# Query projection and expert stage of a PEER feed-forward: five top-16 searches at another place, and pair sums searched among 112 candidates instead of 256

## The chip, the cores and the metric

One core of one Trainium2 chip. The metric is the time of one execution on the device in microseconds (us), taken as the median of several runs. The engines are TensorE (PE, with its weight loads as PEld), VectorE (DVE), ScalarE (ACT), GpSimd (POOL) and SyncE (SP, which issues transfers). Each works through its own instructions in the order in which the program emitted them.

## The reference, cut to what matters

A small network on 512 tokens of width 1024: a Mamba-2 layer, then a sliding-window attention layer, each followed by a PEER feed-forward and a gated embedding. The change is inside the PEER feed-forward, which runs twice:

```python
q = (h @ q_w).reshape(T, 8, 2, 128)                    # 8 heads, two halves
s = einsum('thcd,ckd->thck', q, sub_keys)              # 128 scores for each half
s1, i1 = top_k(s[:, :, 0], 16); s2, i2 = top_k(s[:, :, 1], 16)
cand_s = (s1[..., :, None] + s2[..., None, :])         # 16 x 16 pair sums
best_s, best_pos = top_k(cand_s.reshape(..., 256), 16)
idx = i1[best_pos // 16] * 128 + i2[best_pos % 16]     # 16 experts of 16384, for each head
gate = softmax(best_s)
a = einsum('nd,nhkd->nhk', h, u[idx]); w = gate * gelu(a)
out = einsum('nhk,nhkd->nd', w, v[idx])
```

Both lists s1 and s2 come out sorted, largest first.

## The kernel before, in words

Tokens are in four tiles of 128 (tile 0 to 3). For tile 0 the experts' rows are fetched one by one ("gather"): 128 rows of u and 128 rows of v for each token. For tiles 1 to 3 the whole table of 16384 experts is gone through in 128 **steps** (loop at the end of `peer`): step j streams 128 experts' weights, multiplies them with the 384 tokens (24 matmuls of 128x384, each product in three passes over high and low parts), applies gelu and writes the result GA. A later loop of 128 steps does the same with v.

A streamed weight block comes by SP's transfer (`ahead`, L150), ACT writes its high part `whi` (L169) and POOL its low part `wlo` in four pieces of 256 columns (L172); this is done two blocks ahead.

**Query projection.** 16 columns c of 128 outputs, two for each head. In the round of column c the program emits `lin`, a normalization step `napply` for rounds 3 to 11 (DVE `nf` L760, ACT `hhi` L764; eight of them on DVE, the last in round 10), the score matmuls of the column before (L971) with ACT's copies into `early` (tiles 0 and 3) and `late` (tiles 1 and 2), one call of `step()`, and ACT's copy of the column (`ga`, L966). `step()` takes the next item of the background generator, `bg_topk`: as soon as both halves of head h are there, in round 2h+2, the searches of tiles 0 and 3 for that head. In the odd rounds it has nothing to do.

**A search** (`topk`, `top16`) on DVE: for both halves MAX8, FIND_INDEX8, MATCH_REPLACE8, MAX8, FIND_INDEX8 over 128 columns, then one add that forms the 256 pair sums `cand` (L805), then the same five over them.

**Background of the expert steps** (`bg`). A list of items in a fixed order: T is a search (price 6.0), D a decode of one tile's positions into expert numbers (0.3, 5.0, 5.0 and 0.8), G one onehot (1.5): for four tokens two 128x1024 products on DVE, `early` (L884) and `og` (L886), and one item later 8 small matmuls and a copy (`gmm`, L898, L899). Each of the 128 steps adds 2.65 to a credit, and items are emitted while it is positive. Before, the walk through the list emits the last onehot in step 106.

**Gather.** The decode of tile 0 gives the row numbers `eg`; when two more items have been emitted (`late` is 2), `gi` is set to 0, and from the next step on each step makes 1.17 gather steps: DVE multiplies a fetched row with the activations (L678) and POOL issues the fetch of the row four ahead (L695), on the same queue as the `wlo` pieces. Five row buffers are in turn use. Before, the first gather step is in step 7.

PE waits for DVE in two ways: directly, where `gmm` needs a onehot, and through POOL, where a row's fetch waits until DVE has used the buffer and `wlo` pieces stand behind it.

Of the kernel before, what the change touches and what calls it, by code (L numbers as in the profile page):

```python
# [11 lines left out]
F32 = _mybir.dt.float32  # L12
# [3 lines left out]
U32 = _mybir.dt.uint32  # L16
AF = _mybir.ActivationFunctionType
OP = _mybir.AluOpType
AX = _mybir.AxisListType

P = 128
NT = 512
D = 1024
# [7 lines left out]
NJ = HEADS * TOPK  # L31
LAG = 4
LOP = 4
PAIR = (5, 6)
QT = 4
GSCALE = 32768.0
# [26 lines left out]
class Net:  # L63
# [576 lines left out]
    def peer(self, L):  # L640
# [106 lines left out]
        with ExitStack() as ctx:  # L747
# [46 lines left out]
            def topk(jobs):  # L794
                v = {}
                one, two = [], []
                for n, (tt, hd) in enumerate(jobs):
                    v[n] = mp.tile([P, 2, TOPK], F32, name=f"tv{n}")
                    for c in range(2):
                        src = early[hd][:, first.index(tt), c] if tt in first else late[:, later.index(tt), hd, c]  # L800
                        one.append((src, v[n][:, c, :], idx[:, c, tt, hd, :]))
                top16(one)
                for n, (tt, hd) in enumerate(jobs):
                    cand = mp.tile([P, TOPK, TOPK], F32, name=f"cand{n}", bufs=1)
                    vt.tensor_tensor(cand, v[n][:, 0, :, None].to_broadcast([P, TOPK, TOPK]),  # L805
                                     v[n][:, 1, None, :].to_broadcast([P, TOPK, TOPK]), op=OP.add)
                    two.append((cand.rearrange("p a b -> p (a b)"), best[:, tt, hd, :], pos[:, tt, hd, :]))
                top16(two)

            HK = HEADS * TOPK  # L810
# [5 lines left out]
            def decode_g(tt):  # L816
                gt = mp.tile([P, HEADS, TOPK], F32, name="gt", bufs=1)
                vt.tensor_tensor(gt, best[:, tt], best[:, tt, :, 0:1].to_broadcast([P, HEADS, TOPK]), op=OP.subtract)
                dec[tt] = gt, []
                return lambda: nc.scalar.activation(gt, gt, AF.Exp, scale=self.rv[:, tt:tt + 1])  # L820

            def decode_i(tt, c):
                pi = mp.tile([P, HEADS, TOPK], U32, name="pi", bufs=1)
                if c == 0:
                    vt.tensor_single_scalar(pi, pos[:, tt], 4, op=OP.logical_shift_right)
                else:
                    vt.tensor_single_scalar(pi, pos[:, tt], 15, op=OP.bitwise_and)
                pb = mp.tile([P, TOPK, HEADS], F16, name="pb", bufs=1)
                vt.tensor_copy(pb, pi.rearrange("p h k -> p k h"))
                ib = mp.tile([P, TOPK, HEADS], F16, name="ib")  # L830
                vt.tensor_copy(ib, idx[:, c, tt].rearrange("p h a -> p a h"))
                eq = mp.tile([P, TOPK, HK], F16, name="eq", bufs=1)
                vt.tensor_tensor(eq.rearrange("p a (n q) -> p a n q", q=QT),  # L833
                                 fl(pb).rearrange("p (n q) -> p n q", q=QT)[:, None].to_broadcast([P, TOPK, HK // QT, QT]),
                                 i16[:, :, None, :].to_broadcast([P, TOPK, HK // QT, QT]), op=OP.is_equal)
                e4 = eq.rearrange("p a (k h) -> p a k h", h=HEADS)
                vt.tensor_tensor(e4, e4, ib[:, :, None, :].to_broadcast([P, TOPK, TOPK, HEADS]), op=OP.mult)  # L837
                n = TOPK // 2
                while n > 1:
                    vt.tensor_tensor(eq[:, :n], eq[:, :n], eq[:, n:2 * n], op=OP.add)  # L840
                    n //= 2
                f = mp.tile([P, HK], F32, name=f"fi{c}", bufs=1)
                vt.tensor_tensor(f, eq[:, 0], eq[:, 1], op=OP.add)
                dec[tt][1].append(f)

            def decode_e(tt):
                gt, fi = dec.pop(tt)
                sm = mp.tile([P, 2, HEADS], F32, name="sm")
                vt.tensor_reduce(sm[:, 0], gt, axis=AX.X, op=OP.add)
                vt.reciprocal(sm[:, 1], sm[:, 0])  # L850
                gk = mp.tile([P, TOPK, HEADS], F32, name="gk", bufs=1)
                vt.tensor_tensor(gk, gt.rearrange("p h k -> p k h"), sm[:, 1, None, :].to_broadcast([P, TOPK, HEADS]),
                                 op=OP.mult)
                if tt == 0:
                    ef = wg[:, 0]
                    vt.tensor_scalar(ef, fi[0], float(P), float(L * NBLK * P), op0=OP.mult, op1=OP.add)
                    vt.tensor_tensor(ef, ef, fi[1], op=OP.add)
                    vt.tensor_copy(eg, ef)
                    vt.tensor_copy(gate, fl(gk))

                def turn():
                    if tt == 0:
                        self.gi = 0
                        return
                    pt = self.bank(7)
                    for j, src in enumerate(fi + [fl(gk)]):
                        nc.tensor.transpose(pt[:, j * P:(j + 1) * P], src, self.ident)
                    ts = slice(tt * P - NG, (tt + 1) * P - NG)
                    two = lambda j: pt[:, j * P:(j + 1) * P, None].to_broadcast([P, P, 2])
                    for j in range(2):  # L870
                        nc.scalar.activation(iT[:, ts, j], two(j), AF.Copy)
                    nc.scalar.activation(gT[:, ts, 0], two(2), AF.Copy, scale=GSCALE)
                    vt.scalar_tensor_tensor(gT[:, ts, 1], two(2), GSCALE, gT[:, ts, 0], op0=OP.mult, op1=OP.subtract)
                return turn
# [29 lines left out]
            def bg_topk():  # L904
                done = 0
                for hd in range(HEADS):
                    while self.hready <= hd:
                        yield
                    topk([(tt, hd) for tt in first])
                    yield  # L910

            def bg():
                items = []

                def T(tt, *hds):
                    for hd in hds:
                        items.append((6.0, lambda hd=hd: topk([(tt, hd)])))

                def D(tt):
                    items.append((0.3, lambda: decode_g(tt), 2))  # L920
                    items.append((5.0, lambda: decode_i(tt, 0)))
                    items.append((5.0, lambda: decode_i(tt, 1)))
                    items.append((0.8, lambda: decode_e(tt), 2))

                def G_(tt, lo, hi):
# [2 lines left out]
                        return lambda: gmm(b, o)  # L928
                    for b in range(32 * tt + lo, 32 * tt + hi):
                        items.append((1.5, lambda b=b: one(b)))  # L930
                D(0), T(1, 0, 1), D(3), T(1, 2, 3, 4), G_(3, 0, 12), T(1, 5, 6), G_(3, 12, 20), T(1, 7), D(1)
                G_(3, 20, 28), T(2, 0), G_(3, 28, 32), T(2, 1), G_(1, 0, 4), T(2, 2), G_(1, 4, 8), T(2, 3)
                G_(1, 8, 12), T(2, 4), G_(1, 12, 16), T(2, 5), G_(1, 16, 20), T(2, 6), G_(1, 20, 22), T(2, 7), D(2)
                G_(1, 22, 32), G_(2, 0, 32)
# [622 lines left out]
```

## Time and profile before

| what | us |
|---|---|
| median of 3 runs | 3457.02 (3456.63 to 3461.01) |
| the profiled execution, its own time | 3453.39 |
| its span, first to last instruction | 3451.6 |
| busy in the span: PE, DVE, POOL, ACT | 3291.1, 2672.6, 1953.3, 1455.2 |
| mean granted TensorE clock | 0.983 of full speed |
| first layer: query projection | 540 to 645 |
| first layer: expert steps (u) | 645 to 1283 |
| first layer: second expert loop (v) | 1285 to 1840 |
| second layer: projection, expert steps | 2100 to 2205, 2205 to 2845 |

The profiled execution is 3.6 us under the median. Line numbers (L805) are those of the kernel before. "Busy" of PE counts overlapping matmuls, so its share is no measure of its peak. Times in rows count from the start of the span.

### The profile page before, as it was taken

What the parts mean: (1) busy time and instruction counts of PE and PEld (TensorE: products, weight loads), DVE (VectorE), ACT (ScalarE), POOL (GpSimd) and SP (SyncE); (2) the same over time, 40 slices, a digit from 0 to 9 for tenths busy, and PEclk for the clock granted to TensorE, in tenths of its full rate; (3) what the DMA queues carried; (4) which work ended last, traced back from release to release, by engine and by line L of the source; (5) the groups of instructions that cost most, each with busy time, mean ns of one, the idle gap of its engine ahead of it and who ended that gap; (6) DMA issues with size and microseconds to landing.
All of it is one profiled execution on the core that took longest, in us unless ns stands there. A gap on an engine that the chain in (4) does not pass through costs nothing.

```text
span 3451.6 us, 52253 instructions
## 1 busy us (share of the span) xinstructions
PE 3291.1 (95%) x18814; PEld 3022.6 (88%) x18814; DVE 2672.6 (77%) x4880; ACT 1455.2 (42%) x2198; POOL 1953.3 (57%) x2168
## 2 busy tenths in 40 slices
PE   8999999989999999999998999999999999999997
PEld 5777777989998989999996668989998989999996
DVE  7667667899998737878777865899988737877775
ACT  4433434444445533333334553444445533333334
POOL 5444545789888884322217226688888884322214
PEclk9999999999999999999999999999999999999998
DMA  3222212488888999999983112488888989999982
GB/s 119 85 77 70 74 62 75 151 280 309 309 312 303 330 310 358 358 336 346 337 286 107 45 59 89 138 278 308 316 309 297 334 304 356 353 346 339 339 304 85
DMA packets 357300, 827.50 MB, mean 240 GB/s; under 512 B 30000, under 2 KB 196528, under 8 KB 350896
## 3 DMA queue, kind: packets, MB, share of 16 engines
q1 hardware_dynamic: 235136, 448.59, 40.3%
q0 software_dynamic: 73728, 268.47, 21.1%
q10 hardware_dynamic: 48176, 107.10, 8.2%
q8 instruction: 147, 2.41, 0.3%
q14 instruction: 113, 0.93, 0.1%
HBM read 717.09 MB, written 106.95 MB: 239 GB/s over the span
## 4 chain that ended last, share of the span: by engine, by line
PE 58%; DVE 25%; POOL 7%; issue 5%; DMA 4%; ACT 1%; SPq 0%; POOLq 0%; DVEq 0%; ACTq 0%
PE bank L202 17%; PE bank L203 17%; PE bank L204 17%; POOL wlo L172 6%; DVE row L678 4%; DVE early L884 3%; DVE og L886 2%; DMA row<-u,eg 2%; POOL row L695 2%; DVE eq L840 1%; PE bank L898 1%; DMA wraw<-ut 1%; PE bank L971 1%; DVE eq L833 1%; DVE eq L837 1%
## 5 line engine op out<-in xcount | busy, mean ns | idle before, releaser
L172 POOL TENSOR_TENSOR wlo<-wraw,whi 128x256 fp32r<-128x256 f32 x1564 | 1256.1, 835 | 564.4 <-ACT whi L169 513.1
L169 ACT ACTIVATE whi<-wraw 128x1024 fp32r<-128x1024 f32 x647 | 685.5, 1061 | 740.5 <-issue 316.3
L695 POOL DMA_INDIRECT row<-v,eg x256 | 310.0, 1211 | 716.8 <-DVE yg L687 700.2
L204 PE MATMUL bank<-hhi,wlo 128*128 128x384 f32 x2048 | 699.8, 342 | 13.3 <-POOL wlo L172 13.2
L202 PE MATMUL bank<-hhi,whi 128*128 128x384 f32 x2048 | 708.6, 346 | 0.7 <-ACT whi L169 0.7
L203 PE MATMUL bank<-hlo,whi 128*128 128x384 f32 x2048 | 697.3, 340 | 0.0
L203 PE MATMUL bank<-vlo,whi 128*128 128x384 f32 x2032 | 684.1, 337 | 6.1 <-DVE vlo L744 6.0
L202 PE MATMUL bank<-vhi,whi 128*128 128x384 f32 x2032 | 684.8, 337 | 0.8 <-ACT vhi L742 0.8
L204 PE MATMUL bank<-vhi,wlo 128*128 128x384 f32 x2032 | 683.6, 336 | 0.0
L172 DVE TENSOR_TENSOR wlo<-wraw,whi 128x1024 fp32r<-128x1024 f32 x256 | 313.3, 1224 | 148.6 <-ACT whi L169 147.5
L204 PEld LDWEIGHTS bank<-hhi,wlo 128*128 128x128 f32 x2048 | 392.0, 191 | 20.0 <-POOL wlo L172 19.8
L202 PEld LDWEIGHTS bank<-hhi,whi 128*128 128x128 f32 x2048 | 393.3, 192 | 1.0 <-ACT whi L169 1.0
L203 PEld LDWEIGHTS bank<-hlo,whi 128*128 128x128 f32 x2048 | 392.8, 192 | 0.0
L203 PEld LDWEIGHTS bank<-vlo,whi 128*128 128x128 f32 x2032 | 382.6, 188 | 8.2 <-DVE vlo L744 8.2
L202 PEld LDWEIGHTS bank<-vhi,whi 128*128 128x128 f32 x2032 | 382.6, 188 | 2.0 <-ACT vhi L742 1.5
L204 PEld LDWEIGHTS bank<-vhi,wlo 128*128 128x128 f32 x2032 | 382.4, 188 | 0.3 <-POOL wlo L172 0.3
L678 DVE SCALAR_TENSOR_TENSOR row<-row,pair 128x1024 f32<-128x1024 f32 x256 | 305.6, 1212 | 88.1 <-DMA row<-u,eg 87.6
L687 DVE SCALAR_TENSOR_TENSOR yg<-row,wg,yg 128x1024 f32<-128x1024 f32 x254 | 328.0, 1291 | 35.9 <-DMA row<-v,eg 35.8
L202 PE MATMUL bank<-z,whi 128*128 128x512 f32 x728 | 322.0, 442 | 3.4 <-DVE sg L1137 3.4
L695 POOL DMA_INDIRECT row<-u,eg x256 | 278.5, 1088 | 50.4 <-issue 29.1
L993 ACT ACTIVATE ga<-bank 128x384 f32<-128x384 f32 x256 | 125.3, 490 | 418.0 <-PE bank L204 409.0
L203 PE MATMUL bank<-z,whi 128*128 128x512 f32 x728 | 291.1, 400 | 4.7 <-DVE z L262 4.7
(322 smaller groups left out, 4863.6 us busy)
## 6 DMA issues: line engine op xcount, KB each, us to landing
wraw<-ut SPq DMA_DIRECT2D x256, 512.0 KB
wraw<-v SPq DMA_DIRECT2D x256, 512.0 KB
wraw<-wlin SPq DMA_DIRECT2D x135, 512.0 KB
GA<-ga ACTq DMA_DIRECT2D x256, 192.0 KB
G<-gsz ACTq DMA_DIRECT2D x48, 1024.0 KB
gv<-G SPq DMA_DIRECT2D x96, 512.0 KB
gsz<-GA SPq DMA_DIRECT2D x256, 192.0 KB
PJ<-nf ACTq DMA_DIRECT2D x16, 256.0 KB
```

The source lines that it names most:

```text
L169: nc.scalar.activation(hi, r, AF.Copy)
L172: self.lo_eng.tensor_tensor(lo[:, q:q + n], r[:, q:q + n], hi.bitcast(F32)[:, q:q + n], op=OP.subtract)
L202: mm(out, whi, xhi, start=start, stop=False)
L203: mm(out, whi, xlo, start=False, stop=False)
L204: mm(out, wlo, xhi, start=False, stop=stop)
L678: vt.scalar_tensor_tensor(r, r, 1.0, self.pair, op0=OP.mult, op1=OP.mult, accum_out=wg[:, 0, j:j + 1])
L687: vt.scalar_tensor_tensor(yg, r, wg[:, 0, j:j + 1], yg, op0=OP.mult, op1=OP.add)
L695: nc.gpsimd.indirect_dma_start(out=got[i], out_offset=None, in_=t["u"] if i < NJ else t["v"].rearrange("a p d -> (a p) d"), in_offset=bass ...
L833: vt.tensor_tensor(eq.rearrange("p a (n q) -> p a n q", q=QT), fl(pb).rearrange("p (n q) -> p n q", q=QT)[:, None].to_broadcast([P, TOPK, ...
L884: vt.tensor_tensor(pairs(o), iota.rearrange("p (a d) -> p a d", d=2)[:, None, None].to_broadcast([P, QT, 2, P // 2, 2]), alike(iT), op=OP. ...
L886: vt.tensor_tensor(pairs(og), pairs(o)[:, :, 0:1].to_broadcast([P, QT, 2, P // 2, 2]), alike(gT), op=OP.mult)
L993: nc.scalar.activation(ga[:, NG:], ps[:, NG:], AF.Gelu)
```

## The change

The pair sums are formed for the first four entries of the first list with all 16 of the second (64), and for the other twelve with the first four of the second (48): 112 columns from two adds instead of 256 from one. A position is then decoded differently, with one more DVE instruction in either half of a decode. In the query projection, the rounds after the searches of heads 2 to 6 search one head (0 to 4) of tile 1. The background list of the expert steps loses these five searches and begins with the decodes of tiles 0 and 3. Prices and credit stay.

```diff
+QEARLY = 5
...
-                    cand = mp.tile([P, TOPK, TOPK], F32, name=f"cand{n}", bufs=1)
-                    vt.tensor_tensor(cand, v[n][:, 0, :, None].to_broadcast([P, TOPK, TOPK]),
-                                     v[n][:, 1, None, :].to_broadcast([P, TOPK, TOPK]), op=OP.add)
-                    two.append((cand.rearrange("p a b -> p (a b)"), best[:, tt, hd, :], pos[:, tt, hd, :]))
+                    cand = mp.tile([P, 4 * TOPK + 4 * (TOPK - 4)], F32, name=f"cand{n}", bufs=1)
+                    for a, m, w in ((0, 4, TOPK), (4, TOPK - 4, 4)):
+                        o = cand[:, TOPK * a:TOPK * a + m * w].rearrange("p (a b) -> p a b", b=w)
+                        vt.tensor_tensor(o, v[n][:, 0, a:a + m, None].to_broadcast([P, m, w]),
+                                         v[n][:, 1, None, :w].to_broadcast([P, m, w]), op=OP.add)
+                    two.append((cand, best[:, tt, hd, :], pos[:, tt, hd, :]))
...
+                pb = mp.tile([P, TOPK, HEADS], F16, name=f"pb{c}", bufs=1)
+                turned = lambda x: x.rearrange("p h k -> p k h")
                 if c == 0:
+                    pk = mp.tile([P, HEADS, TOPK], U32, name="pk", bufs=1)
                     vt.tensor_single_scalar(pi, pos[:, tt], 4, op=OP.logical_shift_right)
+                    vt.tensor_single_scalar(pk, pos[:, tt], 2, op=OP.logical_shift_right)
+                    vt.scalar_tensor_tensor(pb, turned(pk), -12.0, turned(pi), op0=OP.add, op1=OP.max)
+                    dec[tt][2].append(pb)
                 else:
-                    vt.tensor_single_scalar(pi, pos[:, tt], 15, op=OP.bitwise_and)
-                pb = mp.tile([P, TOPK, HEADS], F16, name="pb", bufs=1)
-                vt.tensor_copy(pb, pi.rearrange("p h k -> p k h"))
+                    pa, pm = dec[tt][2][0], pi.bitcast(F32).rearrange("p h k -> p (h k)").rearrange(
+                        "p (k h) -> p k h", h=HEADS)
+                    vt.tensor_scalar(pm, pa, 4.0, 48.0, op0=OP.mult, op1=OP.add)
+                    vt.scalar_tensor_tensor(pm, pa, 16.0, pm, op0=OP.mult, op1=OP.min)
+                    vt.tensor_tensor(pb, turned(pos[:, tt]), pm, op=OP.subtract)
...
                     topk([(tt, hd) for tt in first])
                     yield
+                    if 2 <= hd < 2 + QEARLY:
+                        topk([(1, hd - 2)])
+                        yield
...
-                D(0), T(1, 0, 1), D(3), T(1, 2, 3, 4), G_(3, 0, 12), T(1, 5, 6), G_(3, 12, 20), T(1, 7), D(1)
+                D(0), D(3), T(1, 5, 6), G_(3, 0, 12), T(1, 7), G_(3, 12, 20), D(1)
                 G_(3, 20, 28), T(2, 0), G_(3, 28, 32), T(2, 1), G_(1, 0, 4), T(2, 2), G_(1, 4, 8), T(2, 3)
                 G_(1, 8, 12), T(2, 4), G_(1, 12, 16), T(2, 5), G_(1, 16, 20), T(2, 6), G_(1, 20, 22), T(2, 7), D(2)
                 G_(1, 22, 32), G_(2, 0, 32)
```

## Rows read from the trace of the kernel before

**Rows 1.** Busy us of each engine in three stretches of the expert steps; clock, DMA last.

```profile
645.00:1190.00 545.00, 507.65 (x3330) 494.73 (x3329) 508.61 (x964) 271.45 (x338) 476.26 (x544) 0.97 0.86 297
1190.00:1285.00 95.00, 90.91 (x512) 86.75 (x511) 32.30 (x44) 33.85 (x45) 84.12 (x103) 1.00 0.91 315
...
2205.00:2756.00 551.00, 515.40 (x3381) 502.75 (x3380) 497.50 (x971) 275.64 (x343) 483.58 (x552) 0.97 0.85 299
```

**Rows 2.** The chain that ended last, by line, from 645 to 868 us.

```profile
by line: DVE row L678 17.5%; DVE early L884 13.6%; DVE eq L840 7.1%; DVE og L886 6.9%; DVE eq L837 3.9%; DVE eq L833 3.6%; PE bank L202 3.0%; PE bank L204 2.8%; PE bank L203 2.8%; DVE idx L790 2.4%; PE bank L898 2.4%; DVE pos L787 2.2%; DVE
```

**Rows 3.** DVE in order of time, first layer (start us, us, engine line op).

```profile
651.76 0.63 DVE L818 TENSOR_TENSOR gt<-best 128x128 f32<-128x128 f32 x1
...
672.48 0.47 DVE L786 MAX8 tv<-gv 128x8 f32<-128x128 f32 x2
...
683.56 0.27 DVE L818 TENSOR_TENSOR gt<-best 128x128 f32<-128x128 f32 x1
...
699.10 1.22 DVE L678 SCALAR_TENSOR_TENSOR row<-row,pair 128x1024 f32<-128x1024 f32 x1
...
703.69 0.47 DVE L786 MAX8 tv<-gv 128x8 f32<-128x128 f32 x2
...
708.86 1.20 DVE L678 SCALAR_TENSOR_TENSOR row<-row,pair 128x1024 f32<-128x1024 f32 x1
...
1185.62 1.04 DVE L886 TENSOR_TENSOR og<-early,gT 128x1024 f16<-128x1024 f16 x1
```

**Rows 4.** ACT's gelu at the end of steps 14, 15, 20, 22, 107, 108, 127.

```profile
700.86 0.49 ACT L993 ACTIVATE ga<-bank 128x384 f32<-128x384 f32 x1 [2.15 <-PE bank L204]
709.29 0.49 ACT L993 ACTIVATE ga<-bank 128x384 f32<-128x384 f32 x1 [6.39 <-PE bank L204]
...
730.42 0.49 ACT L993 ACTIVATE ga<-bank 128x384 f32<-128x384 f32 x1 [2.15 <-PE bank L204]
...
748.41 0.49 ACT L993 ACTIVATE ga<-bank 128x384 f32<-128x384 f32 x1 [3.11 <-PE bank L204]
...
1189.31 0.49 ACT L993 ACTIVATE ga<-bank 128x384 f32<-128x384 f32 x1 [2.28 <-PE bank L204]
...
1193.47 0.49 ACT L993 ACTIVATE ga<-bank 128x384 f32<-128x384 f32 x1 [2.15 <-PE bank L204]
...
1279.54 0.49 ACT L993 ACTIVATE ga<-bank 128x384 f32<-128x384 f32 x1 [0.81 <-PE bank L204]
```

**Rows 5.** DVE groups by form, 645 to 1190 us; L301 is of the whole span.

```profile
L786 DVE MAX8 tv<-gv 128x8 f32<-128x128 f32 x32 | 7.7, 280 | 0.0
L786 DVE MAX8 best<-cand 128x8 f32<-128x256 f32 x18 | 7.6, 427 | 0.5
L805 DVE TENSOR_TENSOR cand<-tv 128x256 f32<-128x256 f32 x18 | 10.0, 560 | 0.0
L825 DVE TENSOR_SCALAR pi<-pos 128x128 uint32<-128x128 uint32 x4 | 2.0, 488 | 0.0
L678 DVE SCALAR_TENSOR_TENSOR row<-row,pair 128x1024 f32<-128x1024 f32 x115 | 136.8, 1211 | 3.4 <-DMA row<-u,eg 3.4
...
L301 DVE TENSOR_TENSOR rst<-rst 128x4 f32<-128x4 f32 x30 | 4.9, 163 | 1.0
```

**Rows 6.** The shortest kind of that add, in DVE's order of time, and POOL's pieces of `wlo`.

```profile
706.03 0.40 DVE L805 TENSOR_TENSOR cand<-tv 128x256 f32<-128x256 f32 x1
...
L172 POOL TENSOR_TENSOR wlo<-wraw,whi 128x256 fp32r<-128x256 f32 x1564 | 1256.1, 835 | 564.4 <-ACT whi L169 513.1
```

**Rows 7.** DVE in the query projection: two heads' first search instructions, and the normalization between.

```profile
592.21 0.68 DVE L786 MAX8 tv<-early 128x8 f32<-128x128 f32 x3 [2.16 <-ACT early L976]
...
601.63 1.12 DVE L760 SCALAR_TENSOR_TENSOR nf<-x,cols,rs 128x384 f32<-128x384 f32 x2
...
605.44 0.68 DVE L786 MAX8 tv<-early 128x8 f32<-128x128 f32 x3 [2.16 <-ACT early L976]
```

**Rows 8.** POOL's first row fetch, first layer.

```profile
673.34 1.11 POOL L695 DMA_INDIRECT row<-u,eg  x1 [0.16 <-DVE idx L787]
```

More of the change, by code (lines that the diff above doesn't have):

```diff
@@ L818, in decode_g @@
                 vt.tensor_tensor(gt, best[:, tt], best[:, tt, :, 0:1].to_broadcast([P, HEADS, TOPK]), op=OP.subtract)
-                dec[tt] = gt, []
+                dec[tt] = gt, [], []
                 return lambda: nc.scalar.activation(gt, gt, AF.Exp, scale=self.rv[:, tt:tt + 1])
@@ L846, in decode_e @@
             def decode_e(tt):
-                gt, fi = dec.pop(tt)
+                gt, fi, _ = dec.pop(tt)
                 sm = mp.tile([P, 2, HEADS], F32, name="sm")
```

## The prediction

> **What bounds the kernel now.** I read the stage table first, then the chain, then DVE's and ACT's order of time. PE looks full everywhere, but the table [rows 1] shows where it waits for something else: from 645 to 1190 us DVE is busy 508.6 of 545 us and PE's clock is below full (0.97, the mark of short stops), while from 1190 to 1285 DVE needs 32 of 95. In the second layer it is the same, a little less tight (497.5 of 551). The chain of the first 220 us runs through DVE's lines in turn, PE's have a tenth [rows 2]. In DVE's order of time nothing separates its instructions: from the first decode at 651.76 to the last onehot at 1186.6 [rows 3] it always has something waiting. So up to the last onehot DVE sets the end. After it, the steps run without background.
>
> PE's own pace is read from the gelu at the end of each step [rows 4]: a step without onehots takes 4.16 us (1189.31 to 1193.47); step 15 took 8.43, steps 21 and 22 together 18.0. PE does not wait for searches or decodes as such, it pays for DVE's arrears when it meets a late onehot or a late weight block. The last 20 steps take 90.2 us, 4.51 each (1189.31 to 1279.54).
>
> **The change part by part**, for one layer; both layers run the same code.
>
> *Five searches leave the expert steps.* Those of heads 0 and 1 took 672.48 to 683.56, 11.1 us; the next took 703.69 to 708.86, 5.17, and two more the same: 26.6 us off DVE [rows 3].
>
> *Eleven searches stay and get shorter.* MAX8 takes 280 ns over 128 columns and 427 over 256 [rows 5], 1.15 ns a column, so 144 columns fewer save 0.165 us; I take the other four of the five for alike: 0.83. The add becomes two. Its shortest row is 0.40 us [rows 6], an add of 4 columns takes 0.163 [rows 5], so one of 64 has 0.22 and one of 48 0.20 if nothing is in the way. In this stretch the add has a mean of 0.56, 0.16 over its shortest; giving each new one that wait, the two cost 0.74, 0.18 more. Saved: 0.65 a search, 7.2 in all. Without any wait it would be 0.80 and 8.8.
>
> *Four decodes have two instructions more each*, of 128 columns. The nearest row is a decode's shift, 0.488 [rows 5]: 1.0 a decode, 3.9 in all. The bounds are nothing, if the replaced conversions waited more, and twice that.
>
> *The five searches on DVE in the projection.* Two searches, two normalization steps and the wait for the next scores make a cycle of 13.23 us (592.21 to 605.44), of which 2.2 to 2.4 is waiting [rows 7]: PE's two columns set it. Now 1.3 goes (two searches), 4.7 comes (a search of 5.3 less 0.65): 16.6, less what closes of the wait, so 14.2 to 16.6, and I take 15. A normalization step stands behind the added search only for heads 2 and 3, because the eighth and last is in round 10. ACT's `hhi` waits for it, and behind `hhi` on ACT stand the copies to `early`, `ga` and `whi`, for which the score matmuls and POOL wait. Weights are two blocks ahead, 13 us, which hides 3.6 us (two cycles of 1.8 too much); if that cover were gone, PE would lose those 3.6. For heads 4 to 6 the cycle is about even. The last pair of searches saves 1.3, so DVE comes to the first decode 2.3 later. Bounds: 1.3 earlier, 4.5 later.
>
> *Rows.* The gather now begins in step 5, not 7. On POOL the first fetch [rows 8] moves ahead of two blocks' `wlo` pieces and waits there for the row numbers, which DVE has at the end of the first decode (672.48, now 675.8). POOL would come to it about 8.3 us earlier, so two blocks are held up for some 10 us, two steps of which are in reserve: PE stops for 2 to 4 us near step 8. I count nothing, because DVE has the longer queue at the first onehot; without that cover it costs these 4. On SP only the first loads of G start earlier, with the end of the background, beside steps that have DMA at 0.91 already [rows 1].
>
> *The order.* The list loses 30 of its credit, and the walk through it at 2.65 a step emits the last onehot in step 95, not 106. Until then 91 instead of 100 steps gather, 106 rows instead of 117: 11 fewer of 1.21 us [rows 5], 13.3 off DVE's stretch.
>
> *Sum.* DVE's last onehot comes 26.6 + 7.2 - 3.9 - 2.3 + 13.3 = 40.9 us earlier, but PE is then 11 steps less far. Eleven steps without background cost 11 x 4.16 = 45.8 at the pace of a quiet step, 49.6 at the mean of the last 20; I take the quiet one, since the longer ones belong to transfers and v rows which either kernel has. So +4.9 a layer, +9.8 in all. The searches that left were cheap: each bought 6.0/2.65 = 2.26 steps of PE's time, 9.4 us, with 5.3 of its own and 3.2 of rows. What DVE gains becomes idle time behind the last onehot, because prices and credit did not move.
>
> The sum is a difference in the profiled execution (3453.39 us, 3.6 under the median); put on the median 3457.02 it gives **3466.8 us**, slower by 0.28%. Differences under 0.2%, 6.9 us, can hardly be told from none.
>
> **The rivals.**
>
> *The front clears, faster.* Steps 15, 21 and 22 cost 26.4 us where three quiet steps are 12.5: 13.9 of arrears, but for a few small matmuls [rows 4]. If DVE reaches the first onehot in time, now in step 12, both layers save up to 27.8 us, and the sum becomes 3439. It decides at about 697, when PE ends step 13. For it: two searches now stand between the second decode and the first onehot, not five. Against: first decode to 675.8, second (15.5 to the next row, and 1.2 of rest after it [rows 3], 1.0 added) to 693.5, two searches of 4.7 to 702.9, five rows to 709. That is 12 late, as before.
>
> *Waits that do not come, no change.* If the added instructions hardly wait (searches save 8.8, decodes cost 2.0) and the projection stays in step (1.3 earlier), DVE gains 48.0 and the layer loses 45.8: 3457.0 - 4.4 = 3452.6. For it: the singles at 703.69 had an add of 0.40 [rows 6].
>
> *POOL in the way, slower still.* The same add takes 0.40 or, in the mean, 0.56, and MAX8 keeps to its length [rows 5, 6]: the add meets something that MAX8 does not. If the second add of each search always finds a `wlo` piece begun, it waits 0.835 [rows 6] in place of 0.16, 7.4 more over eleven: +12.3 a layer, 3481.6. For it: POOL is busy 476 of 545 us [rows 1]. Against: searches whose add took 0.40 while pieces ran. The Trainium skill, "SBUF — State Buffer", section "SBUF: two separate sides", says that VectorE and GpSimd share a port pair as an exclusive lock for a whole instruction, which an instruction with two SBUF inputs needs against a GpSimd op that reads SBUF, and that the loser fully blocks. By that rule every add, not a share of them, waits whenever POOL holds the port, and the sum would be this rival's; the rows of one add show some that waited and some that did not.
>
> *All freed time counts.* If steps without background cost nothing extra, 26.6 + 7.2 - 3.9 comes off twice: 3397. The 4.16 us of a quiet step speak against it.
>
> **How the numbers follow.** The forecast has 0.41, the clearing front 0.20, the missing waits 0.20, POOL in the way 0.15, all freed time 0.04. The forecast's own bounds are 3455 (missing waits halfway) to 3481. The range leaves out the last rival and the half of the first that comes out lower than its 3439, and goes a little over the slowest: 3438 to 3484. Faster by over 0.2% (under 3450.1): 0.20 + 0.04 and 0.02 of the missing waits, 0.26. Within 0.2%: 0.18 of the missing waits and 0.08 of the forecast's low end, 0.26. Slower: 0.33 + 0.15, 0.48.
>
> **What would show it.** Right: DVE without a gap up to its last onehot, which ends near 1146 us after a first decode at 654; the step then is 96, and 31 steps follow in 135 to 140 us, with DVE idle two thirds of the time. A single search takes about 4.7. Projection still 105 us. POOL's first fetch waits for `eg`. Steps 12 to 14 hold a stop of some 8 us or more. Wrong: a first onehot that PE does not wait for, gaps in DVE before the last onehot (then the steps have another bound, and cheaper searches are worth less than counted), or steps after it well above 4.5 us, which would make it slower than forecast. If the stop at the decodes of tiles 1 and 2 shrinks as well, DVE was never as full as its busy share says, and the time falls below the old one.

## The result, and the profile after

The changed kernel takes **3476.09 us** (median of 5 runs, 3472.01 to 3480.0) beside 3457.02 for the kernel before (5 runs, 3453.1 to 3462.66). The ratio is 1.0053, with a 95% interval of [1.0037, 1.0069]: slower by half a per cent, 19.1 us where 9.8 were forecast. The profiled execution has a span of 3472.3 us (3451.6 before) and nearly the same mean clock (0.984, before 0.983).

First the table by stage, as in [rows 1], with the projection ahead of it and both layers.

```profile
540.00:643.00 103.00, 102.34 (x523) 86.48 (x523) 85.27 (x515) 39.12 (x90) 50.94 (x68) 1.00 0.26 79
643.00:1147.00 504.00, 468.37 (x3069) 454.35 (x3068) 452.37 (x856) 254.44 (x316) 434.25 (x488) 0.97 0.84 295
1147.00:1290.00 143.00, 133.40 (x746) 127.60 (x744) 50.42 (x64) 48.60 (x66) 127.59 (x158) 1.00 0.89 305
...
2226.00:2723.00 497.00, 454.22 (x3003) 440.60 (x3002) 448.10 (x805) 249.10 (x308) 428.92 (x479) 0.97 0.85 295
2723.00:2865.00 142.00, 135.99 (x761) 132.07 (x760) 49.18 (x65) 49.20 (x67) 128.67 (x160) 0.99 0.90 310
```

The stretch with background is shorter (504 us, 545 before), the one without is longer (143, 95 before). DVE's share of the first fell from 0.93 to 0.90. The mark of the stops, a clock of 0.97, stayed.

DVE in order of time: the first decode, the row numbers of tile 0, and the last onehot of the first layer, then the first decode and the last onehot of the second.

```profile
652.58 0.28 DVE L821 TENSOR_TENSOR gt<-best 128x128 f32<-128x128 f32 x1
...
669.96 0.23 DVE L869 CAST eg<-wg 128x128 int32<-128x128 f32 x1
...
1142.17 1.05 DVE L897 TENSOR_TENSOR og<-early,gT 128x1024 f16<-128x1024 f16 x1
...
2226.41 0.27 DVE L821 TENSOR_TENSOR gt<-best 128x128 f32<-128x128 f32 x1
...
2718.36 1.19 DVE L897 TENSOR_TENSOR og<-early,gT 128x1024 f16<-128x1024 f16 x1
```

ACT's gelu at the end of steps 6, 7, 8, 13, 14, 96, 97 and 127 (as [rows 4]).

```profile
666.14 0.49 ACT L1007 ACTIVATE ga<-bank 128x384 f32<-128x384 f32 x1 [1.97 <-PE bank L205]
673.22 0.49 ACT L1007 ACTIVATE ga<-bank 128x384 f32<-128x384 f32 x1
678.90 0.49 ACT L1007 ACTIVATE ga<-bank 128x384 f32<-128x384 f32 x1 [3.67 <-PE bank L205]
...
702.37 0.49 ACT L1007 ACTIVATE ga<-bank 128x384 f32<-128x384 f32 x1 [1.00 <-PE bank L205]
711.76 0.49 ACT L1007 ACTIVATE ga<-bank 128x384 f32<-128x384 f32 x1 [3.19 <-PE bank L205]
...
1145.71 0.49 ACT L1007 ACTIVATE ga<-bank 128x384 f32<-128x384 f32 x1 [1.91 <-PE bank L205]
1149.95 0.49 ACT L1007 ACTIVATE ga<-bank 128x384 f32<-128x384 f32 x1 [2.23 <-PE bank L205]
...
1288.36 0.47 ACT L1007 ACTIVATE ga<-bank 128x384 f32<-128x384 f32 x1
```

The last onehot ends at 1143.2 in step 96, and 31 steps follow, 1145.71 to 1288.36, 142.7 us (138.7 in the second layer). From the first gelu to the last the loop takes 645.6 us (634.9 before); in the second layer 646.3 (634.2). These 10.7 and 12.1 us are all of the loss (the span is 20.7 us longer).

Where do they arise? The same gelu times, taken by groups of steps, show it (first layer, us; the four kernels on the right are experiments, below).

| steps | before | after | before, rate 2.40 | after, rate 2.15 | before, 2.40, grid matmul later | after, 2.15, grid matmul later |
|---|---|---|---|---|---|---|
| 0 to 8 | 31.3 | 36.2 | 31.3 | 32.5 | 31.3 | 32.5 |
| 8 to 24 | 82.3 | 85.8 | 69.6 | 85.1 | 69.7 | 81.1 |
| 24 to 96 | 368.0 | 381.0 | 358.0 | 345.1 | 344.2 | 346.1 |
| 96 to 118 | 111.1 | 97.5 | 126.1 | 116.8 | 119.8 | 108.3 |
| 118 to 127 | 42.2 | 45.2 | 39.2 | 42.1 | 40.8 | 42.1 |

Steps 96 to 118 gain 13.6, since no onehot is left there. But steps 24 to 96 lose 13.0: they now hold 80 onehots in place of 69. The front, where the first onehot now stands in step 14 and not in step 20, loses 8.4 (16 onehots in steps 0 to 24 in place of 8), the end 3.0. One execution of each kernel was profiled. In e2 below the second layer's loop took 12 us longer than the first layer's, at a median that is no different from the kernel before. So a difference of a few us between groups of steps is a hint and no more. What the groups say is that the background was packed into fewer steps; that it got no cheaper for PE when it got cheaper for DVE is what the experiments have to show.

The waits say the same. First those of the kernel before, 645 to 1190 us (what waited, for what: us in total, times, longest), which the prediction did not look at:

```profile
PE bank L898 <- DVE og L886: 33.4, 19, 3.2
...
DVE og L886 <- PE bank L898: 19.3, 15, 3.4
```

Then after, 643 to 1147:

```profile
PE bank L909 <- DVE og L897: 31.2, 15, 3.2
...
DVE og L897 <- PE bank L909: 24.9, 17, 3.4
DVE row L679 <- DMA row<-u,eg: 14.2, 7, 3.9
```

PE waits for onehots nearly as long as before, though DVE has some 32 us of searches less. And DVE waits for PE in turn, in the kernel before already: `og` has two buffers, so DVE can't write the third before PE has used the first. Each stands still while the other is late.

Here is one such stop in the changed kernel, from the timelines of DVE, POOL, PE and ACT (start, duration, engine, line), with the stretch behind it from the table by stage.

```profile
947.57 1.22 DVE L679 SCALAR_TENSOR_TENSOR row<-row,pair 128x1024 f32<-128x1024 f32 x1 [3.94 <-DMA row<-u,eg]
...
948.72 0.73 DVE L895 TENSOR_TENSOR early<-iota,iT 128x1024 f16<-128x1024 f16 x1
949.55 3.47 DVE L897 TENSOR_TENSOR og<-early,gT 128x1024 f16<-128x1024 f16 x1
...
949.69 2.77 POOL L173 TENSOR_TENSOR wlo<-wraw,whi 128x256 fp32r<-128x256 f32 x4
...
953.07 0.61 PE L909 MATMUL bank<-og,early 128*128 128x128 f16 x8 [3.14 <-DVE og L897]
...
955.64 0.52 PE L205 MATMUL bank<-hhi,wlo 128*128 128x384 f32 x1
...
949.96 0.49 ACT L1007 ACTIVATE ga<-bank 128x384 f32<-128x384 f32 x1 [2.15 <-PE bank L205]
959.53 0.49 ACT L1007 ACTIVATE ga<-bank 128x384 f32<-128x384 f32 x1 [3.88 <-PE bank L205]
...
954.40:957.20 2.80, 2.80 (x10) 2.80 (x9) 2.70 (x5) 1.25 (x2) 1.47 (x2) 0.50 0.98 392
```

DVE first waits 3.94 us for a fetched row. Then the onehot product, 0.69 us where no piece of `wlo` runs beside it, takes 3.47 and ends 0.56 behind a run of four pieces on POOL. PE reaches the small matmuls and stands for 3.14 us. Then for some 3 us its granted clock is 0.50 of full speed, 1.2 in place of 2.4 GHz, and its matmuls of 384 columns take 0.52 in place of 0.34. The step lasts 9.6 us. The late row may have a part in it, since without that wait the onehot would have been begun earlier; no run shows how it would have come out.

### The profile page after: what moved, and what is told of

It is laid out like the page before. It is cut to its first block, busy times and chain, and to the rows that moved or that the text cites. A ratio compares the mean times of both kernels' runs of the same rounds, so it can differ in the third digit from the quotient of the medians.

```text
span 3472.3 us, 52333 instructions
## 1 busy us (share of the span) xinstructions
PE 3303.7 (95%) x18814; PEld 3032.2 (87%) x18814; DVE 2630.3 (76%) x4960; ACT 1456.3 (42%) x2198; POOL 1968.2 (57%) x2168
## 4 chain that ended last, share of the span: by engine, by line
PE 57%; DVE 24%; POOL 8%; DMA 6%; issue 4%; ACT 1%; SPq 0%; POOLq 0%; DVEq 0%; ACTq 0%
PE bank L203 17%; PE bank L204 17%; PE bank L205 17%; POOL wlo L173 6%; DVE row L679 3%; DMA row<-u,eg 3%; DVE early L895 2%; DVE og L897 2%; POOL row L696 2%; DMA wraw<-ut 1%; DVE eq L851 1%; PE bank L909 1%; DVE cand L808 1%; DVE eq L848 1%; DVE idx L788 1%
## 5 line engine op out<-in xcount | busy, mean ns | idle before, releaser
L696 POOL DMA_INDIRECT row<-v,eg x256 | 320.9, 1254 | 692.0 <-DVE yg L688 679.4
L205 PE MATMUL bank<-z,wlo 128*128 128x512 f32 x728 | 291.4, 400 | 0.0
```

The source lines that it names most:

```text
L205: mm(out, wlo, xhi, start=False, stop=stop)
L696: nc.gpsimd.indirect_dma_start(out=got[i], out_offset=None, in_=t["u"] if i < NJ else t["v"].rearrange("a p d -> (a p) d"), in_offset=bass ...
```

## The experiments

Theory A is the prediction's: DVE's amount of work sets when the last onehot ends, and the steps behind it come on top. Theory B: that amount doesn't bind; the credit places the end, and PE pays for stops. Theory C is B made definite, after the first runs: the number of uncovered steps, plus the stops at the onehots. Line numbers of edits on the kernel before are its own.

| kernel | last onehot in step | median us | ratio to before, 95% interval |
|---|---|---|---|
| e5_before_rate296 | 96 | 3483.54 | 1.0079 [1.0054, 1.0105] |
| e1_move_only | 95, 96 | 3496.36 | 1.0112 [1.0087, 1.0137] |
| the changed kernel | 96 | 3476.09 | 1.0053 [1.0037, 1.0069] |
| e2_cand_only | 107 | 3455.84 | 0.9992 [0.9982, 1.0001] |
| e3_after_rate237 | 107 | 3450.84 | 0.998 [0.9969, 0.9992] |
| e4_before_rate240 | 118 | 3429.06 | 0.9913 [0.9888, 0.9938] |
| e6_after_rate215 | 118 | 3428.94 | 0.9908 [0.9877, 0.9939] |
| e7_after_late2 | 96, 97 | 3447.85 | 0.9965 [0.9947, 0.9983] |
| e8_after_gather7 | 96 | 3472.33 | 1.0045 [1.003, 1.006] |
| e9_after_rate215_late2 | 118 | 3410.95 | 0.9867 [0.9843, 0.989] |
| e10_before_rate240_late2 | 118 | 3399.03 | 0.9827 [0.9803, 0.9851] |
| e11_after_u_only | 96 | 3457.63 | 0.9999 [0.9982, 1.0015] |
| e12_after_lop8 | 96 | 3574.24 | 1.0343 [1.0315, 1.037] |

**The parts alone.** *The move and the new order, with 256 pair sums and the old decode:*

```diff
+QEARLY = 5
...
+                    if 2 <= hd < 2 + QEARLY:
+                        topk([(1, hd - 2)])
+                        yield
...
-                D(0), T(1, 0, 1), D(3), T(1, 2, 3, 4), G_(3, 0, 12), T(1, 5, 6), G_(3, 12, 20), T(1, 7), D(1)
+                D(0), D(3), T(1, 5, 6), G_(3, 0, 12), T(1, 7), G_(3, 12, 20), D(1)
```

> Only the move and the new order of the list; pair sums over 256 columns and the old decode. Theory A (DVE's queue sets when the last onehot ends, the credit sets in which step, and every step after it costs 4.2 to 4.6 us): against the kernel before, DVE's stretch loses 26.6 (searches) and 13.3 (rows) a layer, but the projection, now 5.3 us longer per added search, sends DVE some 11 us late into the first decode; 11 more steps cost 46 to 52. So +17 to +23 a layer, 3491 to 3503. Rival B (the stretch is held by PE, POOL and transfers, and DVE's queue does not matter): as the changed kernel, about 3476.

Measured 3496.36, +39 on the kernel before. That is in theory A's range and 20 above rival B's figure, so B in this form is wrong: what DVE does counts in the projection and right behind it. The projection falls out of step: from its first score matmul to the first gelu it takes 107.4 and 106.4 us (101.1 in the changed kernel and 101.1 and 101.2 before). The first decode stands 15.2 and 16.6 us behind the first gelu (9.9 in the changed kernel, 7.1 before), and steps 0 to 8 take 41.4 and 41.3 us (36.2 and 33.8). In these two places lies about all of the 20 us between this kernel and the changed one, which has the shorter searches. It leaves open what DVE's work does in the stretch of the onehots, by far the longest.

*112 pair sums and the new decode, nothing moved:* the changed kernel's `topk` and `decode_i`, with the list and the projection of before.

```diff
-                    if 2 <= hd < 2 + QEARLY:
+                    if False:
```

> Only the 112 candidates and the new decode; searches and list where they were. A: 16 searches shorter by 0.65 and the last pair of the projection by 1.3, four decodes longer by 1.0: DVE's stretch 7.8 us shorter a layer, no step moved, so 3441. B: no change, 3457. If the second add and the decodes cost more than counted: up to 3465.

Measured 3455.84, no difference that can be told from none. The searches take 9.0 us less of DVE's time in the first layer and 12.1 in the second, and the loops take 633.2 us (634.9 before) and 645.1 (634.2) in the profiled execution. DVE's saving bought nothing that shows, which is against theory A (3441).

*The earlier end alone:* the kernel before, with a credit that puts the last onehot where the change puts it.

```diff
-URATE, VRATE, BRATE = 1.17, 0.94, 2.65
+URATE, VRATE, BRATE = 1.17, 0.94, 2.96
```

> The kernel before with 2.96 instead of 2.65 credit a step: its last onehot comes in step 95, as in the changed kernel; searches, candidates and list as before. If the earlier end of the background by itself costs the time (denser steps with longer stops, then 31 uncovered steps of 4.5 us): slower than the changed kernel, since its denser steps also hold the five searches: 3485 to 3530. If DVE's queue alone decides (theory A), its stretch only loses 13 us of rows and 11 steps of 4.5 come after it: +36 a layer, 3529. If the cost lies in the moved searches and the new instructions: about 3457.

Measured 3483.54: +26 with no search moved or shortened, 45 under what theory A gave (3529) and a little under the first theory's range. So an earlier end alone costs more than the change loses. Given that end, all that was taken off DVE is worth 7.4 us (3483.54 to 3476.09), and the intervals of the two ratios overlap.

**The end put back.** If DVE's work were the bound, the changed kernel with a slower credit should end much lower than the kernel before at the same step.

```diff
-URATE, VRATE, BRATE = 1.17, 0.94, 2.65
+URATE, VRATE, BRATE = 1.17, 0.94, 2.37
```

> The changed kernel with 2.37 instead of 2.65 credit a step, so that the last onehot is emitted in step 106 again, as before the change. A: DVE's stretch has 25 us a layer less than before with as many steps after it: 3400 to 3415, well under both kernels. B (other bounds hold the steps): no better than before, 3457 to 3476.

Measured 3450.84, 6.2 under the kernel before, whose last onehot is in the same step; theory A wanted some 40 or more. Next both kernels with the end at step 118: the kernel before at 2.40, the changed one at 2.15, by the same line.

> The kernel before with 2.40 instead of 2.65 credit a step: last onehot emitted in step 117 instead of 106, nothing else. A: 11 rows more on DVE (+13 us) and 11 steps fewer after the last onehot (-46 to -52): -33 to -39 a layer, 3380 to 3390, unless the steps come near PE's own pace first (4.16 us and the onehots' matmuls), which allows about 3400. B: 3450 to 3470.

> The changed kernel with 2.15 credit a step: last onehot in step 117, as in the kernel before with 2.40 (3429). Theory A (DVE's work decides): 25 us a layer under that, about 3380. Theory C (what is left are stops of PE that do not depend on DVE's load, 45 to 60 us a layer, and the freed time is idle): 3420 to 3432.

3429.06 and 3428.94: alike, though with a scatter (the runs of the first go from 3417.8 to 3444.4) that could hide some us. Theory A wanted 3380 to 3400 for the first and some 3380 for the second; it fails in the stretch of the onehots, for the size of the gain and for the comparison. Theory C holds. What the lighter DVE does with its time shows in its wait for rows, 50 us in the first layer of e6 and 17 in that of e4 (groups of DVE, line of the row product).

**The stops.** `gmm` (grid matmul) two items after its onehot instead of one, with a third buffer for `og` and a fourth for `early`:

```diff
-                o = mp.tile([P, QT, 2, P], F16, name="early", bufs=3)
-                og = mp.tile([P, QT, 2, P], F16, name="og")
+                o = mp.tile([P, QT, 2, P], F16, name="early", bufs=4)
+                og = mp.tile([P, QT, 2, P], F16, name="og", bufs=3)
...
-                        items.append((1.5, lambda b=b: one(b)))
+                        items.append((1.5, lambda b=b: one(b), 2))
...
-                        early[hd] = mp.tile([P, 2, 2, P], F32, name="early", bufs=3)
+                        early[hd] = mp.tile([P, 2, 2, P], F32, name="early", bufs=4)
```

> The changed kernel with a onehot's matmuls emitted two items after it instead of one (a third og buffer, a fourth early buffer for it). Theory C, in the form that PE's stops come from single onehots which DVE finishes some 3 us late behind a run of POOL's wlo pieces: most of these stops have 2 to 4 us more time and go, with the half-speed clock after them: 3410 to 3440. Theory A: DVE's queue is as long as before and PE meets it one item later: 3470 to 3476.

Measured 3447.85, 28 under the changed kernel, with nothing taken off any engine: theory C's direction, at less than its price (3410 to 3440), and outside theory A's range (3470 to 3476). Its waits, 643 to 1147 us:

```profile
PE bank L909 <- DVE og L897: 13.4, 7, 3.1
DVE row L679 <- DMA row<-u,eg: 10.5, 3, 4.6
...
DVE og L897 <- PE bank L909: 1.8, 2, 1.2
```

PE's wait fell from 31.2 to 13.4 us, DVE's from 24.9 to 1.8.

Then both edits together, on either kernel (`early` keeps its three buffers here; the rate is 2.15 on the changed kernel, 2.40 on the one before):

```diff
-URATE, VRATE, BRATE = 1.17, 0.94, 2.65
+URATE, VRATE, BRATE = 1.17, 0.94, 2.15
...
+                og = mp.tile([P, QT, 2, P], F16, name="og", bufs=3)
...
+                        items.append((1.5, lambda b=b: one(b), 2))
```

> The changed kernel with its credit rate lowered until the last onehot falls at about step 117 (alone: 3429) and with the grid matmul issued two items after its onehot (alone: 3448 against 3476). Theory C (the time is the number of steps that run without background, plus the stops in which TensorE waits for a onehot; VectorE's amount of work doesn't count): both gains add up in part, 3400 to 3422. Theory A (VectorE's work is the bound of the stretch): with the end of the background given by the credit, the grid matmul's place changes nothing, 3425 to 3432.

> The same two edits on the kernel before (last onehot at about step 117; the rate alone gave 3429). Theory C: as the changed kernel with the same two edits, to within 8 us, since the searches that the change takes off VectorE don't set the time. Theory D (once the stops are loosened, VectorE's work decides): 10 to 40 us above the changed kernel with the same edits, as it has about 31 us more of searches in each layer.

3410.95 and 3399.03. Theory D is wrong even in sign: the kernel that has more DVE work is 12 us faster. Theory C has the level of both, but its 8 us between them are exceeded. Waits of the changed kernel with both edits, 643 to 1211:

```profile
DVE row L679 <- DMA row<-u,eg: 31.6, 16, 5.2
...
PE bank L909 <- DVE og L897: 3.6, 3, 1.6
```

And of the kernel before with both, 641 to 1205, where DVE is busy 544.9 of 564 us:

```profile
641.00:1205.00 564.00, 543.59 (x3578) 525.58 (x3577) 544.90 (x989) 287.09 (x359) 523.88 (x596) 1.00 0.89 311
```
```profile
PE bank L898 <- DVE og L886: 14.8, 9, 3.3
...
DVE row L678 <- DMA row<-u,eg: 8.9, 7, 4.0
```

Now DVE is nearly full (0.97), and still this kernel is the fastest of all. The table by steps names the place: steps 0 to 24 take 113.6 us with the searches moved and 101.0 without (114.3 and 100.7 in the second layer). With the searches moved the first onehot stands in step 16 and not in step 22, so more of the background lies in these steps (12 onehots in steps 0 to 24 in place of 4), and the later ones give back 8.3 of the 12.6. So the searches that stay in the list may be good filling: DVE's work in steps in which PE needs no onehot. That is an argument, no run shows it.

**The front.** The changed kernel with its gather again begun in step 7:

```diff
-                    items.append((0.8, lambda: decode_e(tt), 2))
+                    items.append((0.8, lambda: decode_e(tt), 3 if tt == 0 else 2))
```

> The changed kernel with the gather begun in step 7 again, after the decode of tile 0 has ended, not in step 5. If the stop of POOL at the first row fetch near step 8, and the two more steps with v rows at the end, are worth what they show: 3 to 6 us a layer, 3464 to 3470. If DVE's arrears at the first onehot swallow the first: about 3473 to 3476.

Measured 3472.33, 4 lower, with intervals that overlap: not told apart from none, and between the two forecasts. In the first layer steps 0 to 8 take 33.7 in place of 36.2, but steps 72 to 96 take 144.8 (137.2).

**The long onehot products.** `wlo` in eight pieces of 128 columns:

```diff
-LOP = 4
+LOP = 8
```

> The changed kernel with the low weight part converted in eight pieces of 128 columns rather than four of 256. Theory F (a onehot operation on VectorE, once it has to wait for GpSimd, waits for the whole run of pieces that stand ready): the 3.4 us operations stay as long or get longer, and GpSimd's conversion costs more in all: 3476 to 3500. Rival G (it gets in between two pieces): the long operations fall under 1.5 us and the stops with them: 3440 to 3465.

Measured 3574.24, 98 over the changed kernel, far more than theory F gave (3476 to 3500) and no gain as in G. Of the onehot products 45 take over 2 us, 38 in the changed kernel; G is wrong. POOL's group, 639 to 1181, and the longest product beside its run of pieces, from the timelines of DVE and POOL:

```profile
L173 POOL TENSOR_TENSOR wlo<-wraw,whi 128x128 fp32r<-128x128 f32 x752 | 375.1, 534 | 37.2 <-ACT whi L170 35.9
```
```profile
765.23 4.17 DVE L895 TENSOR_TENSOR early<-iota,iT 128x1024 f16<-128x1024 f16 x1
...
765.47 3.38 POOL L173 TENSOR_TENSOR wlo<-wraw,whi 128x128 fp32r<-128x128 f32 x8
```

Eight pieces of 0.534 and one fetch of 1.07 are 5.3 us a step (as a sum of means), where a step of this stretch takes 5.6 (542 us for 96), so POOL has little room left; and PE's wait for onehots rises to 46.2 us. The products still wait out whole runs. How the 98 us divide between POOL's greater work and these waits isn't separated, so F rests on the durations and not on the time.

**The uncovered steps.** The gather of the first loop stops after its last u row, so that no v row is multiplied there:

```diff
-URATE, VRATE, BRATE = 1.17, 0.94, 2.65
+URATE, VRATE, BRATE = 1.17, 1.06, 2.65
...
-                gather(URATE)
+                if self.gi is None or self.gi < NJ + LAG:
+                    gather(URATE)
```

> The changed kernel without the v rows in the u loop: the gather stops after the last u row, and the v loop does all of its own. Theory E (the product of the row with gelu reads two tiles in SBUF and holds up GpSimd's weight pieces, 0.90 to 0.97 us each beside 0.74; it lengthens the uncovered steps): some eight steps of each layer become 0.7 shorter, but the v loop starts with its first rows not ready and may lose that again: 3462 to 3474. Rival: the uncovered steps are set by the weights' DMA alone, and the v loop's start is later: 3476 to 3490.

Measured 3457.63: 18 us less, more than theory E's range has; its rival is wrong. POOL's pieces in the uncovered steps, of the changed kernel (1147 to 1290):

```profile
L173 POOL TENSOR_TENSOR wlo<-wraw,whi 128x256 fp32r<-128x256 f32 x123 | 94.9, 805 | 8.8 <-ACT whi L170 8.3
```

and of this one (1145 to 1280), with the chain that ended last there:

```profile
L173 POOL TENSOR_TENSOR wlo<-wraw,whi 128x256 fp32r<-128x256 f32 x128 | 90.1, 737 | 14.6 <-ACT whi L170 14.3
...
by line: PE bank L205 21.3%; PE bank L204 21.0%; PE bank L203 20.9%; DMA wraw<-ut 11.8%; POOL wlo L173 9.4%; issue 8.4%; DMA G<-gsz 7.5%; POOL row L696 2.4%; ACT gsz L910 0.8%; ACT ga L1007 0.4%; SPq L715 0.3%; ACTq L1008 0.2%; POOLq L173 0
```

In the changed kernel the same chain runs through POOL's pieces (37.1%, shown below); here 63% of it are PE's own matmuls. The pieces that were long are those beside a v row's product: the 11 that overlap one in the uncovered steps of the changed kernel's first layer take 1.47 us in the mean, the 64 with no DVE instruction beside them 0.74. That is theory E's mechanism. The edit also takes the v rows' fetches off POOL and the DMA engines in these steps, so how much of the gain is due to the products alone isn't shown.

The 31 uncovered steps take 133.3 us here (4.30 each) and 142.7 in the changed kernel. The two loops with u give 8.2 and 5.4 of the gain in the profiled executions; the higher v rate of the loops with v comes with it and was not tried alone.

## Why the prediction was right, and where it was not

**The time and the sign** were right: 3476.1 lies in the range, on the forecast's side, at twice its size. It lies nearer to the rival "POOL in the way" (3481.6) than to the forecast (3466.8). That the time came out right is in part luck, since two terms of the sum were wrong in opposite directions (below).

**The events** came as told. First decode 652.6 (654 forecast), last onehot 1143.2 (1146), step 96, 31 steps in 142.7 and 138.7 us (135 to 140). POOL's first fetch waits: it stands 3.51 us and starts at 670.47, right behind `eg`. The projection takes what it took: from the first head's cycle of 14.73 us (590.59 to 605.32; 15 taken) to the first gelu at 642.7, and the first decode is 2.8 later against it (2.3). A single search takes 4.95 in the mean of eleven in the first layer, 4.83 in the second (4.7 forecast). The adds cost more than estimated, since they wait like the old one:

```profile
L808 DVE TENSOR_TENSOR cand<-tv 128x64 f32<-128x64 f32 x13 | 7.7, 589 | 0.0
...
L808 DVE TENSOR_TENSOR cand<-tv 128x48 f32<-128x48 f32 x13 | 5.4, 412 | 0.0
```

In the second layer they have means of 348 and 451 ns, which is about the 0.74 for both. The rival "POOL in the way" asked for more, a second add that always waits: of the 48-column adds of the eleven searches, 3 in the first layer and 5 in the second take some 0.75, the others 0.20 or 0.21.

The reading that spoke against this rival, an add of 0.40 "while pieces ran", was wrong for the add that was shown. At 706.03 no piece ran; POOL was at a row fetch between two runs of pieces:

```profile
702.81 2.92 POOL L172 TENSOR_TENSOR wlo<-wraw,whi 128x256 fp32r<-128x256 f32 x4
705.89 0.95 POOL L695 DMA_INDIRECT row<-u,eg  x1 [0.16 <-issue]
706.87 2.80 POOL L172 TENSOR_TENSOR wlo<-wraw,whi 128x256 fp32r<-128x256 f32 x4
```

Of the first layer's 18 adds [rows 5], ten took 0.40 to 0.42, seven of them with no piece beside them; the eight that took 0.61 to 0.88 all had a piece begun before them. Of the eleven that started beside a running piece, eight waited; so what an add costs is mostly a matter of how often it meets one.

**The step that failed** is the first reading: "from the first decode [...] to the last onehot [...] it always has something waiting. So up to the last onehot DVE sets the end." The trace of before had 36.4 us of DVE idle in that stretch of the first layer, 27.9 of it ahead of `og` (19.3 of this in waits for PE) and 3.4 ahead of rows; the rows quoted were those in which nothing separates the instructions. What the runs show in its place: where the last onehot ends is set by the credit, which says after how many steps it comes, and by the stops that DVE and PE give each other on the way. That the last onehot came 41.5 us earlier against the first gelu, nearly as the sum said (40.9), is no proof of its terms (in the second layer it was 37.0). The shorter searches alone, tried in e2, moved nothing that shows in the time; an end 11 steps sooner, tried alone in e5, cost more than the whole change. There the last onehot comes 31.9 us earlier (510.1 against 542.0 us after the first gelu; 30.1 in the second layer) without one search removed or shortened, where the sum had only the 13.3 of the rows for fewer steps. What is left for the searches, the decodes and the projection is 9.6 us (6.9 in the second layer), where the sum had 26.6 + 7.2 - 3.9 - 2.3 = 27.6. Two errors of some 18 us each cancelled, and that is the luck.

**The mis-sized terms.** Eleven uncovered steps were put at 45.8, at the pace of a quiet step. They cost 52.4 in the first layer (31 steps in 142.65 less 20 in 90.23) and 47.1 in the second. The mean of the last 20 steps, 49.6, which the text set aside, was nearer. It chose the quiet step because "the longer ones belong to transfers and v rows which either kernel has". But a longer tail has more of such steps: the eleven cost 4.77 and 4.28 us each, where 4.16 were taken. The chain of waits there (1147 to 1290) names POOL's pieces, the weights' transfers and the row fetch:

```profile
by line: POOL wlo L173 37.1%; DMA wraw<-ut 21.1%; issue 13.4%; DMA row<-u,eg 13.1%; POOL row L696 9.4%; DMA wraw<-v 3.4%; DVE row L679 2.6%; DVE wg L692 0.5%; DVE wg L683 0.2%; POOLq L173 0.2%; POOLq L696 0.1%
```

And POOL's detour at the first fetch, counted at nothing behind DVE's queue with "it costs these 4" as the other end, is seen: steps 0 to 8 are 4.9 longer in the first layer and 2.5 in the second. Steps 7 and 8 hold it (7.1 and 5.7 us).

**The rivals.** The front did not clear: the stop of "some 8 us or more" is there, 9.4 in step 14. "All freed time counts" (3397) is refuted by the time, and by e6 against e4: even with the same end, the freed time is worth nothing that shows. "Waits that do not come" (3452.6) is refuted by the time: adds waited, and the first decode came later against the first gelu, not earlier. The sentence on what would make the prediction wrong, gaps in DVE before the last onehot, came true for the mechanism though the time held.

**Open.** Why the front costs more with the searches moved than its later steps return (e9 against e10) was read from the steps, not tried. That the delay of a kernel's onehots works through the stops rests on e7 and on the waits; the delay and the extra buffers were not tried apart. Nor was the credit of e9 fitted again, or e11's edit put on the kernel before.

## What to carry to other kernels

Work that is handed out by a credit has three sides to keep apart: what it costs its own engine, where the credit puts it, and the stops that it gives the engine it runs beside. When items leave such a list, fit the rate again before judging the change; a rate alone was worth 28 us on the kernel before, and an item's delay with more buffers 28 on the changed one, both without any work saved. A busy share of 0.93 is no proof of a bound: read the waits in both directions between the two engines first.

## What the runs showed of the hardware

A DVE product of two SBUF tiles can be held up by far more than one POOL instruction. Counted in the trace of the changed kernel, 137 of its 384 onehot products have no `wlo` piece beside them and take 0.69 us in the mean; 122 that overlap two take 1.04; 26 that overlap a run of four take 3.33. A longer product overlaps more pieces by its length alone, but the ends tell which waits for which: each of these 26 ends 0.55 or 0.56 us behind the end of its fourth piece, as does the one shown (952.46 and 953.02). With eight pieces of half the size 30 products overlap all eight and take 3.62. The Trainium skill, "SBUF — State Buffer", section "SBUF: two separate sides", says of the port pair of these two engines that whoever starts first has it for the whole instruction and the other fully blocks. The waits agree with a block, but the length of one instruction does not cover them: with pieces of 0.53 us a product lasted 4.17. Nor does the recorded order of starts: 17 of the 26 start, by their rows, 0.01 to 0.24 us before the first of the four pieces, like the one shown (949.55 and 949.69). Why some get in after one piece and others behind the whole run, no run here shows.

It also goes the other way. A v row's product, with its row, the weight and the sum in SBUF, stretches the pieces beside it (1.47 us in the mean against 0.74, above); a u row's product, whose second tile is in PSUM, doesn't: 41 pieces beside such products in the same steps take 0.74.

PE's granted clock is lower where it stops longer, though not strictly in that order: in the first layer's stretch with background it is 0.93 in e12 (46.2 us of PE's waits for onehots; PE is busy 475.9 of 542 us), 0.97 in the kernel before and after (33.4 and 31.2), 0.99 in e9 (3.6) and 1.00 in e10 (14.8).
